# First attention of a float32 transformer: output projection in two parts, heads 0 to 5 and heads 6 to 7, with the attention's items in the order of the heads

## The chip, the cores and the metric

The kernel runs on one core of one Trainium2 chip, as one program. The metric is the time of an execution on the device, in microseconds (us); lower is better. The engines of the core are named as the profile names them: PE (TensorE, matrix products and transposes), DVE (VectorE), ACT (ScalarE), POOL (GpSimd), and SP, whose queue issues most of the transfers of weights.

## The reference, cut to what matters

A first block of two layers (a convolution layer, then an attention layer) is followed by a second block. All is float32, 512 positions of 1024 channels. The change lies in the attention layer of the first block: eight heads, each with two sets of scores whose softmaxes are subtracted; the 128 outputs of each head are normalised by their own root mean square; then comes the product with `w_o`, whose result is normalised again, scaled and added to x.

```python
    def one_block(args):                       # one of 4 blocks of 128 query positions
        ...
        s = jnp.einsum("bqhcd,bkhcd->bhcqk", q_blk, k).astype(jnp.float32) * scale + bias[None, :, None]
        s = jnp.where(rel >= 0, s, -jnp.inf)
        p = jax.nn.softmax(s, axis=-1)
        a = (p[:, :, 0] - lam * p[:, :, 1]).astype(v.dtype)
        return jnp.einsum("bhqk,bkhe->bqhe", a, v)
    o = lax.map(one_block, (q, starts))
    o = jnp.moveaxis(o, 0, 1).reshape(bsz, seq, N_HEADS, V_HEAD_DIM)
    o = rms_norm(o, subln_g) * (1.0 - lambda_init)
    return o.reshape(bsz, seq, N_HEADS * V_HEAD_DIM) @ w_o
...
        x = x + g_m * rms_norm(y, norm_g[l, 1])
        h = rms_norm(x, norm_g[l, 2]) * (1.0 + sc_f) + sh_f
        y = conv_ffn(h, ffn_w_in[l], ffn_dw[l], ffn_dwb[l], ffn_w_out[l])
```

## The kernel before, in words

Every large product is made of three: both factors are split into a high part and a low part, and `mm3` (L208) issues high by high, low by high and high by low, each 128x128 by 128x512. A weight comes in by a transfer on SP's queue (`wr`), ACT casts its high part (`wh`, L135), and DVE or, for every second piece here, POOL subtracts to get the low part (`wl`, L137).

The attention is a list of 32 items (`todo`), one for each head and query block (`qb`, also called a token block, 0 to 3). `pipeline` goes through it one item per iteration: it issues the scores of item i (`attn1_s`, PE `sc` L1160), then the first half of the filling work, the transposes of the probabilities of item i-2 (`attn1_t`, PE `aT` L1198, copied by ACT to `at`, L1200), the second half of the filling work, and the product with v of item i-4 (`attn1_v`, PE `pv` L1206, written to `o` by ACT L1208, its squares summed by L1209). The scores of item i+1 come next on PE. The statistics of an item are DVE's (maxima, L1170 to L1174), its exponentials are ACT's (L1177, L1179); the combination of the two softmaxes (DVE L1186 to L1190) is issued one iteration later. Query block 3 has four times the columns of query block 0.

The filling work is a list of generators, `fillers`; `fill` advances the first one so many steps per item, as `FILL1` sets it: 4.61, and 5 from item 26 on. A step is one `mm3`. The fillers are first the projections of heads 1 to 7 (`proj`: eight steps for k, whose sum DVE copies to `kq`, L1149, and eight for q, which ACT copies, L1151); then the output projection, `down8`. It takes token blocks 0 to 3 in turn, for each the two halves of the output columns (`acc`), eight steps each, one for each head's 128 channels of `o`.

For a token block whose last head is done, POOL computes the eight roots (`rstd_pool`, L202), and `advance` counts its steps (`age`): at `MULT` DVE multiplies `o` by them (L1259, 128x1024), at `AGE` PE transposes it (`T` in the words below, PE `ps` L351), ACT copies it with the gain (`hf`, L374), and DVE splits it into four pairs of high and low parts (`put`, L367 and L368). The items of heads 6 and 7 are interleaved so that head 7 begins early:

```python
    todo = [(hd, qb) for hd in range(6) for qb in range(4)]
    todo += [(6, 0), (6, 1), (7, 0), (6, 2), (7, 1), (6, 3), (7, 2), (7, 3)]
```

After the product a token block's rows are normalised and added to x (`norm_half` and `norm_end`, L386 to L400), give the new `xr` (L326), and are transposed and evacuated once more (`T` and `E`) as the input of the layer's feed-forward part. For that, x comes back from memory by four transfers of 512 KB (`reload`), issued when the first token block's heads are done.

Of the kernel before, what the change touches and what calls it, by code (L numbers as in the profile page):

```python
# [38 lines left out]
LALD2 = (7, 8)  # L39
LAG1 = (2, 4)  # L40
MID = 2
MULT = 4
FILL1 = (4.61, 5)
AGE = (9, 11, 6, 10, 14, 12, 21, 12)
SEL_RATE = (1.4, 1, 0.6, 0.4, 1.0, 1.3, 1.3, 1.0, 1.2)
SEL_TICK = 4
START_PAIRS = 3
# [644 lines left out]
def program(b, t, out, stop):  # L692
# [277 lines left out]
    def mk_chain(gb):  # L970

        def end(tok, ps):
            b.norm_end(tok, ps, gb())
            xr[tok] = b.xr_of(tok, ss=b.ssx[:, tok, :])
        return (lambda tok, ps: b.norm_half(tok, ps, gb())), end
# [61 lines left out]
    def run_ffn(l, E, h, bg, rate, chain, T2, E2):  # L1037

        units, inter = ffn(l, None)
        b.bg += bg  # L1040
        b.bgrate = rate
        b.start_units(units, h, T, E, first=3)
        b.bgrate *= 2
        b.down(inter, NF, ('fo', l), chain, T2, E2)
# [4 lines left out]
    def E_mod(h, l, ja, js):  # L1049
        def E(tok):  # L1050
            if tok == 0:
                b.finish(f'm{l}{ja}')
                b.finish(f'm{l}{js}')
            b.evac_mod(tp.pop(tok), tok, h, b.mod[l, ja], b.mod[l, js])
        return E
# [175 lines left out]
                    done(j)  # L1231
    for _ in proj(0):
        pass
    todo = [(hd, qb) for hd in range(6) for qb in range(4)]
    todo += [(6, 0), (6, 1), (7, 0), (6, 2), (7, 1), (6, 3), (7, 2), (7, 3)]
    sg = b.C([128, 1], n="sg")
    nc.vector.tensor_scalar(out=sg, in0=b.col('subln'), scalar1=1.0 - LINIT, scalar2=None, op0=ALU.mult)
    age, orr = {}, {}
    h = b.newpair(8)
    E = E_mod(h, 1, 4, 3)  # L1240

    def done(j):
        hd, tok = todo[j]
        if hd < 7:
            return
        if tok == 0:
            holder['oc'] = b.newpair(8)
            b.reload()
            fillers.append(b.down8(holder['oc'], 'wo', mk_chain(lambda: b.mod[1, 2]), T, E, pre=lambda tok: age.get(tok, 0) >= AGE[4 + tok]))
        orr[tok] = b.rstd_pool(oss[tok], 128, 8)  # L1250
        age[tok] = 0

    def advance():

        for tok in age:
            age[tok] += 1
            if age[tok] == MULT:
                oo = o[tok].rearrange("p (h e) -> p h e", e=128)
                nc.vector.tensor_tensor(out=oo, in0=oo, in1=orr[tok].unsqueeze(2).to_broadcast([128, 8, 128]), op=ALU.mult)  # L1259
            if age[tok] == AGE[tok]:  # L1260
                b.evac_gain(b.transp(o[tok]), tok, holder['oc'], sg)
        while fillers:
            try:
                next(fillers[0])
                return
            except StopIteration:
                fillers.pop(0)
# [2 lines left out]
    owed = [0.0]  # L1270

    def fill(i, part):
        owed[0] += FILL1[0] / 2 if i < 26 else FILL1[1] / 2
        while owed[0] >= 1:
            owed[0] -= 1
            advance()
# [12 lines left out]
        b.evac_gain(tp.pop(tok), tok, holder['h2'], ang2)  # L1289
    b.lo_pool = LO_POOL[1]  # L1290
    b.side = rel_bias2(b, t, tab)
    run_ffn(1, E, h, [('rope', rope_tables(b, t))], 1, mk_chain(lambda: b.mod[1, 5]), T, E_b2)
    assert next(b.side, 0) == 0
    b.side = None
    if stop == 'ffn1':
# [456 lines left out]
def rope_tables(b, t):  # L1752

    nc = b.nc
    posi = b.G([128, 512], I32, n="posi")
    nc.sync.dma_start(out=posi, in_=t['positions_2'][0].partition_broadcast(128))
    posf = b.G([128, 512], n="posf")
    nc.vector.tensor_copy(posf, posi)
    rc = b.C([128, 2], n="rc")
    nc.sync.dma_start(out=rc, in_=t['k_rope'])  # L1760
    yield

    ak_ = b.G([128, 2, 512], n="ang")
    ang, kk = ak_[:, 0, :], ak_[:, 1, :]
    nc.vector.tensor_scalar(out=ang, in0=posf, scalar1=rc[:, 0:1], scalar2=None, op0=ALU.mult)
    yield
    MAGIC = 12582912.0
    nc.vector.tensor_scalar(out=kk, in0=ang, scalar1=1.0 / (2 * math.pi), scalar2=MAGIC, op0=ALU.mult, op1=ALU.add)
    yield
    nc.vector.tensor_scalar(out=kk, in0=kk, scalar1=-MAGIC, scalar2=None, op0=ALU.add)  # L1770
    yield
    c1, c2 = 6.28125, 0.0019340515136718750
    c3 = 2 * math.pi - c1 - c2
    for cc in (c1, c2, c3):
        nc.vector.scalar_tensor_tensor(out=ang, in0=kk, scalar=-cc, in1=ang, op0=ALU.mult, op1=ALU.add)
    nc.vector.tensor_scalar(out=ang, in0=ang, scalar1=math.pi, scalar2=-math.pi, op0=ALU.min, op1=ALU.max)
    yield
    trig = b.G([128, 2, 512], n="trig")
    sin_t, cos_t = trig[:, 0, :], trig[:, 1, :]
    nc.scalar.activation(out=sin_t, in_=ang, func=AF.Sin)  # L1780
    yield
    nc.vector.tensor_scalar(out=sin_t, in0=sin_t, scalar1=rc[:, 1:2], scalar2=None, op0=ALU.mult)
    yield
    nc.vector.scalar_tensor_tensor(out=kk, in0=ang, scalar=-1.0, in1=ang, op0=ALU.mult, op1=ALU.max)
    nc.vector.tensor_scalar(out=kk, in0=kk, scalar1=-1.0, scalar2=math.pi / 2, op0=ALU.mult, op1=ALU.add)
    yield
    nc.scalar.activation(out=cos_t, in_=kk, func=AF.Sin)
    yield
    b.trig = sin_t, cos_t
    yield  # L1790
# [150 lines left out]
```

## Time and profile before

| | us |
|---|---|
| runs | 2046.29, 2044.12, 2044.9 |
| median | 2044.9 |
| profiled execution | 2047.63 |
| its span | 2045.9 |

The profile is of one execution, whose own time is the third row; the span is from its first to its last instruction. PE's busy time is 96% of the span, DVE's 62%, ACT's 41%, POOL's 8%, and the mean of the clock granted to PE is 0.984 of full speed. A timeline row gives the start, the duration, the engine, the line, the operation with what it writes and reads, and in square brackets the idle time of the engine ahead of it with what ended that. Where matmuls stand in a row, the duration of one reaches into the next: the starts say how fast they follow each other.

### The profile page before, as it was taken

Reading aid. Unit: us, or ns where it says so; the run is one execution under the profiler, and the core shown is the slowest. Engines: PE = TensorE matmul, PEld = TensorE weight load, DVE = VectorE, ACT = ScalarE, POOL = GpSimd, SP = SyncE. Lnnn points to the kernel's source line nnn. Section 1 sums busy time; section 2 is a strip of 40 time slices with the busy share of each in tenths; the row PEclk is TensorE's granted clock in tenths of the full one; section 3 lists DMA queues with packets and bytes.
Section 4 is the critical chain, followed back from the end, with each engine's and each line's share of the span. In section 5 each row is a group of like instructions: output and inputs, shape, how many; then the busy total and the mean of one; then the engine's idle time right before and its main releaser. Section 6 shows DMA issues by size and latency. Waiting matters only on the chain. (4 is left out here: it accounts for less than half of the span.)

```text
span 2045.9 us, 25689 instructions
## 1 busy us (share of the span) xinstructions
PE 1956.2 (96%) x9616; PEld 1612.2 (79%) x9618; DVE 1273.5 (62%) x2429; ACT 829.8 (41%) x1682; POOL 156.2 (8%) x99
## 2 busy tenths in 40 slices
PE   5999999999999999889999999989999999999998
PEld 3798788777887877678888888867777878888887
DVE  7788667777866665767766633668786646433432
ACT  3310454343424455745444422554445335322421
POOL 1201000000000111110000000022222100000000
PEclk9999899999999999999999999999999999999999
DMA  8375236443665311302932333321114433332221
GB/s 316 115 249 178 78 138 226 132 148 137 227 251 184 116 47 61 136 36 105 252 117 86 97 109 134 117 62 48 46 45 126 161 134 114 114 129 88 82 93 42
DMA packets 85418, 259.47 MB, mean 127 GB/s; under 512 B 9429, under 2 KB 21117, under 8 KB 85290
## 3 DMA queue, kind: packets, MB, share of 16 engines
q1 hardware_dynamic: 77802, 232.63, 34.4%
q10 hardware_dynamic: 7488, 25.17, 3.2%
q8 instruction: 76, 1.25, 0.2%
q14 instruction: 52, 0.43, 0.1%
HBM read 243.04 MB, written 23.64 MB: 130 GB/s over the span
## 5 line engine op out<-in xcount | busy, mean ns | idle before, releaser
L210 PE MATMUL up<-hh,wh 128*128 128x512 f32 (+1 forms) x1280 | 479.8, 375 | 5.2 <-ACT hh L769 2.1
L212 PE MATMUL up<-hh,wl 128*128 128x512 f32 (+1 forms) x1280 | 475.3, 371 | 4.0 <-DVE wl L137 3.8
L211 PE MATMUL up<-hl,wh 128*128 128x512 f32 (+1 forms) x1280 | 475.1, 371 | 1.2 <-DVE hl L771 1.0
L137 DVE TENSOR_TENSOR wl<-wr,wh 128x1024 fp32r<-128x1024 f32 x247 | 301.6, 1232 | 169.8 <-ACT wh L135 144.0
L135 ACT CAST wh<-wr 128x1024 fp32r<-128x1024 f32 (+2 forms) x308 | 307.9, 1020 | 181.9 <-DMA wr<-in_w_all_dram 97.4
L210 PEld LDWEIGHTS up<-hh,wh 128*128 128x128 f32 x1280 | 243.1, 190 | 50.7 <-issue 2.8
L212 PEld LDWEIGHTS up<-hh,wl 128*128 128x128 f32 x1280 | 243.1, 190 | 49.9 <-DVE wl L137 9.1
L211 PEld LDWEIGHTS up<-hl,wh 128*128 128x128 f32 x1280 | 243.1, 190 | 45.2 <-DVE hl L771 3.3
L210 PE MATMUL acc<-wh,ih 128*128 128x512 f32 x608 | 237.4, 390 | 0.0
L211 PE MATMUL acc<-wl,ih 128*128 128x512 f32 x608 | 236.8, 389 | 0.2 <-DVE wl L137 0.2
L212 PE MATMUL acc<-wh,il 128*128 128x512 f32 x608 | 236.6, 389 | 0.0
L137 POOL TENSOR_TENSOR wl<-wr,wh 128x1024 fp32r<-128x1024 f32 (+2 forms) x61 | 131.8, 2166 | 1002.0 <-ACT wh L135 845.7
L211 PEld LDWEIGHTS acc<-wl,ih 128*128 128x128 f32 x608 | 114.2, 188 | 24.3 <-DVE wl L137 0.9
L212 PEld LDWEIGHTS acc<-wh,il 128*128 128x128 f32 x608 | 114.1, 188 | 23.9
L210 PEld LDWEIGHTS acc<-wh,ih 128*128 128x128 f32 x608 | 114.1, 188 | 23.4
L263 DVE SCALAR_TENSOR_TENSOR macc<-mraw,cact,macc 128x1024 f32<-128x1024 f32 x74 | 95.2, 1287 | 8.5 <-DMA mraw<-in_mod_w_dram 7.8
L1028 ACT CAST ih<-fc 128x512 fp32r<-128x512 f32 x44 | 37.9, 861 | 142.7 <-DVE fc L1020 142.7
L996 ACT ACTIVATE fc<-up,cols 128x512 f32<-128x512 f32 x88 | 68.2, 775 | 37.3 <-PE up L212 37.3
L1001 DVE SCALAR_TENSOR_TENSOR fc<-up,cols,fc 128x384 f32<-128x384 f32 (+3 forms) x176 | 72.8, 479 | 4.7 <-ACT fc L996 4.7
L210 PE MATMUL unit<-hh,wh 128*128 128x512 f32 x152 | 72.3, 476 | 0.7 <-ACT kh L1405 0.5
L1012 ACT ACTIVATE fc<-fc 128x512 f32<-128x512 f32 x44 | 27.8, 632 | 102.3 <-DVE fc L1001 61.4
L1029 DVE TENSOR_TENSOR il<-fc,ih 128x512 fp32r<-128x512 f32 x44 | 39.8, 904 | 40.9 <-ACT ih L1028 40.9
(324 smaller groups left out, 3023.3 us busy)
## 6 DMA issues: line engine op xcount, KB each, us to landing
wr<-in_w_all_dram SPq DMA_DIRECT2D x282, 512.0 KB, 3.7
mraw<-in_mod_w_dram SPq DMA_DIRECT2D x80, 512.0 KB, 5.1
xd<-x ACTq DMA_DIRECT2D x20, 512.0 KB, 2.8
x<-xd ACTq DMA_DIRECT2D x20, 512.0 KB, 5.6
mraw<-in_w_all_dram SPq DMA_DIRECT2D x16, 512.0 KB, 9.6
wr<-in_w_all_dram SPq DMA_DIRECT2D x17, 256.0 KB, 2.7
wr<-in_w_all_dram SPq DMA_DIRECT2D x8, 384.0 KB, 9.5
sk<-fd SPq DMA_DIRECT2D x6, 512.0 KB, 15.8
```

The costliest lines, as they stand in the source:

```text
L135: self.nc.scalar.copy(hi, raw)
L137: (self.nc.gpsimd if pool else self.nc.vector).tensor_tensor(out=lo, in0=raw, in1=hi, op=ALU.subtract)
L210: mm(ps, lh, rh, start=start, stop=False)
L211: mm(ps, lh, rl, start=False, stop=False)
L212: mm(ps, ll, rh, start=False, stop=stop)
L263: nc.vector.scalar_tensor_tensor(out=acc, in0=raws[k], scalar=s, in1=acc, op0=ALU.mult, op1=ALU.add)
L996: nc.scalar.activation(out=o, in_=ps, func=AF.Identity, scale=dw[:, 88 + j:89 + j], bias=dwb[:, j:j + 1])
L1001: nc.vector.scalar_tensor_tensor(out=a, in0=e, scalar=dw[:, w + j:w + j + 1], in1=a, op0=ALU.mult, op1=ALU.add)
L1012: nc.scalar.activation(out=o, in_=o, func=AF.Silu)
L1028: nc.scalar.copy(hi, o)
L1029: nc.vector.tensor_sub(lo, o, hi)
```

## The change

The items go head by head. The filling work is 4.0 steps an item, and 3 from item 28 on. The output projection gets a generator of its own, `wo`, in place of `down8`. It is divided by heads: part 0 is heads 0 to 5, six of the eight steps of a sum, part 1 is heads 6 and 7. `WO_ORDER` lists token blocks 0 and 1 with part 0 (both halves of the columns, 24 steps), then their part 1, then token blocks 2 and 3 with all. The roots, the multiply (now at age 3), the transposes (at age 6), the copies and the pairs of a token block are made for each part by itself, for heads 0 to 5 as soon as head 5 is done for that token block. `WO_T` says before which of the parts the transposes of the new `xr` stand, and `h1`, the pair of tiles that they fill, is taken at the first of them. The reload of x is issued two iterations later.

```diff
@@ -39,9 +39,13 @@
 LALD2 = (7, 8)
 LAG1 = (2, 4)
 MID = 2
-MULT = 4
-FILL1 = (4.61, 5)
-AGE = (9, 11, 6, 10, 14, 12, 21, 12)
+MULT = 3
+FILL1 = (4.0, 3)
+HA = 6
+WO_ORDER = [(tok, half, part) for part in range(2) for tok in (0, 1) for half in range(2)]
+WO_T = {(2, 1, 0): 0, (2, 0, 1): 1, (3, 0, 1): 2}
+WO_ORDER += [(tok, half, part) for tok in (2, 3) for part in range(2) for half in range(2)]
+AGE = (6, 9)
 SEL_RATE = (1.4, 1, 0.6, 0.4, 1.0, 1.3, 1.3, 1.0, 1.2)
 SEL_TICK = 4
 START_PAIRS = 3
@@ -1231,34 +1235,86 @@
                     done(j)
     for _ in proj(0):
         pass
-    todo = [(hd, qb) for hd in range(6) for qb in range(4)]
-    todo += [(6, 0), (6, 1), (7, 0), (6, 2), (7, 1), (6, 3), (7, 2), (7, 3)]
+    todo = [(hd, qb) for hd in range(8) for qb in range(4)]
     sg = b.C([128, 1], n="sg")
     nc.vector.tensor_scalar(out=sg, in0=b.col('subln'), scalar1=1.0 - LINIT, scalar2=None, op0=ALU.mult)
     age, orr = {}, {}
-    h = b.newpair(8)
-    E = E_mod(h, 1, 4, 3)
+
+    def E(tok):
+        if tok == 0:
+            b.finish('m14')
+            b.finish('m13')
+            holder['h1'] = b.newpair(8)
+        b.evac_mod(tp.pop(tok), tok, holder['h1'], b.mod[1, 4], b.mod[1, 3])
+
+    def wo():
+
+        la, b.la = b.la, 0
+        ws = [b.get(('wo', 0, k0)) for k0 in range(0, 8, 2)]
+        oc, first, end = holder['oc'], *mk_chain(lambda: b.mod[1, 2])
+        ps = {}
+
+        def seg(tok, half, ks):
+            if ks[0] == 0:
+                ps[tok, half] = b.PS(n="acc")
+            for k in ks:
+                if len(ws) < 8 and k % 2:
+                    ws.append(b.get(('wo', 1, 2 * len(ws) - 8)))
+                w = ws[half * 4 + k // 2]
+                a, e = tok * 128, tok * 128 + 128
+                b.mm3(ps[tok, half], oc.hi(k, a, e), oc.lo(k, a, e), w[0][:, k % 2, :], w[1][:, k % 2, :], k == 0, k == 7)
+                yield
+        for tok, half, part in WO_ORDER:
+            while age.get((part, tok), 0) < AGE[1]:
+                yield
+            if tok == NT - 1 and half and part:
+                b.la = la
+            if tok >= 2 and not half and not part:
+                b.ahead(min(la, tok - 1))
+            if (tok, half, part) in WO_T:
+                T(WO_T[tok, half, part])
+                E(WO_T[tok, half, part])
+            yield from seg(tok, half, range(HA) if not part else range(HA, 8))
+            if part:
+                (end if half else first)(tok, ps.pop((tok, half)))
+        b.ahead()
 
     def done(j):
         hd, tok = todo[j]
-        if hd < 7:
-            return
-        if tok == 0:
-            holder['oc'] = b.newpair(8)
-            b.reload()
-            fillers.append(b.down8(holder['oc'], 'wo', mk_chain(lambda: b.mod[1, 2]), T, E, pre=lambda tok: age.get(tok, 0) >= AGE[4 + tok]))
-        orr[tok] = b.rstd_pool(oss[tok], 128, 8)
-        age[tok] = 0
+        if hd == HA - 1:
+            orr[0, tok] = b.rstd_pool(oss[tok][:, 0:HA], 128, HA)
+            age[0, tok] = 0
+        if hd == 7:
+            orr[1, tok] = b.rstd_pool(oss[tok][:, HA:], 128, 8 - HA)
+            age[1, tok] = 0
+            if tok == 0:
+                b.reload()
+
+    def heads(part, tok):
+        return (0, HA) if not part else (HA, 8)
 
     def advance():
 
-        for tok in age:
-            age[tok] += 1
-            if age[tok] == MULT:
-                oo = o[tok].rearrange("p (h e) -> p h e", e=128)
-                nc.vector.tensor_tensor(out=oo, in0=oo, in1=orr[tok].unsqueeze(2).to_broadcast([128, 8, 128]), op=ALU.mult)
-            if age[tok] == AGE[tok]:
-                b.evac_gain(b.transp(o[tok]), tok, holder['oc'], sg)
+        for part, tok in age:
+            age[part, tok] += 1
+            k0, k1 = heads(part, tok)
+            n = k1 - k0
+            if age[part, tok] == MULT:
+                oo = o[tok][:, k0 * 128:k1 * 128].rearrange("p (h e) -> p h e", e=128)
+                nc.vector.tensor_tensor(out=oo, in0=oo, in1=orr[part, tok].unsqueeze(2).to_broadcast([128, n, 128]), op=ALU.mult)
+            if age[part, tok] == AGE[0]:
+                if (part, tok) == (0, 0):
+                    holder['oc'] = b.newpair(8)
+                    fillers.append(wo())
+                a = slice(tok * 128, tok * 128 + 128)
+                hf = b.G([128, n, 128], n="hf")
+                for q, ps in enumerate(b.transp(o[tok][:, k0 * 128:k1 * 128], n)):
+                    m = min(4, n - 4 * q)
+                    nc.scalar.activation(out=hf[:, 4 * q:4 * q + m, :], in_=ps[:, :m, :], func=AF.Copy, scale=sg)
+                for q in range(n // 2):
+                    hi, lo = holder['oc'].his[k0 // 2 + q][:, :, a], holder['oc'].los[k0 // 2 + q][:, :, a]
+                    nc.vector.tensor_copy(hi, hf[:, 2 * q:2 * q + 2, :])
+                    nc.vector.tensor_sub(lo, hf[:, 2 * q:2 * q + 2, :], hi)
         while fillers:
             try:
                 next(fillers[0])
@@ -1270,7 +1326,7 @@
     owed = [0.0]
 
     def fill(i, part):
-        owed[0] += FILL1[0] / 2 if i < 26 else FILL1[1] / 2
+        owed[0] += FILL1[0] / 2 if i < 28 else FILL1[1] / 2
         while owed[0] >= 1:
             owed[0] -= 1
             advance()
@@ -1289,7 +1345,7 @@
         b.evac_gain(tp.pop(tok), tok, holder['h2'], ang2)
     b.lo_pool = LO_POOL[1]
     b.side = rel_bias2(b, t, tab)
-    run_ffn(1, E, h, [('rope', rope_tables(b, t))], 1, mk_chain(lambda: b.mod[1, 5]), T, E_b2)
+    run_ffn(1, E, holder['h1'], [('rope', rope_tables(b, t))], 1, mk_chain(lambda: b.mod[1, 5]), T, E_b2)
     assert next(b.side, 0) == 0
     b.side = None
     if stop == 'ffn1':
```

The first place is ACT at the end of a head's items. Before, these are the rows around the copy of q of head 4 (`kq_6084`); `p` with 128x256 x2 are the exponentials of query block 1, the rows with 128x128 and 128x256 those of query block 2, `wh` is a weight's cast.

```order
L1179 ACTIVATE p_6210,sm_6209<-p_6210,sm_6208 128x256 x2
L1200 COPY at_6235<-aT_6230 128x512
L1151 ACTIVATE kq_6084<-kp_6183 128x512
L1208 ACTIVATE o_5506<-pv_6244,sm_6019 128x128
L1209 ACTIVATE junk_83,oss_5510<-pv_6244,sm_6019 128x128
L1177 ACTIVATE p_6256,sm_6255<-sc_6249,sm_6254 128x128
L1179 ACTIVATE p_6256,sm_6255<-p_6256,sm_6254 128x256
L1177 ACTIVATE p_6256,sm_6255<-sc_6251,sm_6254 128x128
L1179 ACTIVATE p_6256,sm_6255<-p_6256,sm_6254 128x256
L135 CAST wh_6272<-wr_6089 128x1024
```

After, the rows that end with the copy of q of head 6 (`kq_6518`) begin with the exponentials of query block 2, and those with 128x256 from `sc_6642` and `sc_6644` are of query block 3.

```order
L1181 ACTIVATE p_6598,sm_6597<-sc_6593,sm_6596 128x128
L1183 ACTIVATE p_6598,sm_6597<-p_6598,sm_6596 128x256
L139 CAST wh_6613<-wr_6426 128x1024
L1204 COPY at_6628<-aT_6626 128x128
L1212 ACTIVATE o_5507<-pv_6636,sm_6417 128x128
L1213 ACTIVATE junk_83,oss_5511<-pv_6636,sm_6417 128x128
L1181 ACTIVATE p_6649,sm_6648<-sc_6642,sm_6647 128x256
L1183 ACTIVATE p_6649,sm_6648<-p_6649,sm_6647 128x256
L1181 ACTIVATE p_6649,sm_6648<-sc_6644,sm_6647 128x256
L1183 ACTIVATE p_6649,sm_6648<-p_6649,sm_6647 128x256
L1204 COPY at_6674<-aT_6671 128x256
L1155 ACTIVATE kq_6518<-kp_6619 128x512
```

The copy of q has moved from behind the exponentials of query block 1 to behind those of query block 3, the last item of the head before; the cast stands behind those of query block 2 in both.

The second place is DVE between query blocks 2 and 3 of a head's items. Before (head 4's; `p_6410` is the combination of query block 1):

```order
L1174 TENSOR_SCALAR sm_6459<-sm_6458 128x2
L1187 RECIPROCAL sm_6416<-sm_6409 128x2
L1189 SCALAR_TENSOR_TENSOR sm_6473<-sm_6409,sm_6416,nlam_2173 128x1
L1190 SCALAR_TENSOR_TENSOR p_6410<-p_6410,sm_6473 128x256
L1170 TENSOR_REDUCE sm_6505<-sc_6501 128x1
L1171 ISA p_6508,sm_6505<-sc_6501,bt_5515,sm_6505 128x256
```

After (the items of head 5, with `wl_6614` the low part of a weight):

```order
L1178 TENSOR_SCALAR sm_6596<-sm_6595 128x2
L1191 RECIPROCAL sm_6561<-sm_6554 128x2
L1193 SCALAR_TENSOR_TENSOR sm_6610<-sm_6554,sm_6561,nlam_2173 128x1
L1194 SCALAR_TENSOR_TENSOR p_6555<-p_6555,sm_6610 128x256
L141 TENSOR_TENSOR wl_6614<-wr_6426,wh_6613 128x1024
L1174 TENSOR_REDUCE sm_6646<-sc_6642 128x1
L1175 ISA p_6649,sm_6646<-sc_6642,bt_5515,sm_6646 128x256
```

The low part of a weight now stands between the combination and the maxima of query block 3.

The third place is PE from the first transposes of `o` on. Before, `ps_7055` and `ps_7060` are those of token block 0; the last scores are `sc_6995` and `sc_6997`, and the first product of the output projection is `acc_7092`.

```order
L1160 MATMUL sc_6995<-kq_6619 128x512
L1160 MATMUL sc_6997<-kq_6619 128x512
L1198 MATMUL aT_7030<-ident_71,p_6918 128x128 x4
L1206 MATMUL pv_7038<-v_5087,at_6937 128x128
L1206 MATMUL pv_7038<-v_5088,at_6937 128x128
L1206 MATMUL pv_7038<-v_5089,at_6937 128x128
L1198 MATMUL aT_7049<-ident_71,p_6951 128x128 x3
L351 MATMUL ps_7055<-ident_71,o_5505 128x128 x4
L351 MATMUL ps_7060<-ident_71,o_5505 128x128 x4
L1206 MATMUL pv_7076<-v_5087,at_6970 128x128
L1206 MATMUL pv_7076<-v_5088,at_6970 128x128
L1198 MATMUL aT_7084<-ident_71,p_7002 128x128 x4
L210 MATMUL acc_7092<-wh_6528,hh_6976 128x512
```

After, the transposes of token block 0 (six, for heads 0 to 5) stand in the third item of head 6 (`sc_6789`), and `kp_6817` is head 7's projection:

```order
L1164 MATMUL sc_6789<-kq_6518 128x384
L1164 MATMUL sc_6791<-kq_6518 128x384
L214 MATMUL kp_6817<-hh_5079,wh_6519 128x512
L215 MATMUL kp_6817<-hl_5083,wh_6519 128x512
L216 MATMUL kp_6817<-hh_5079,wl_6520 128x512
L355 MATMUL ps_6830<-ident_71,o_5505 128x128 x4
L355 MATMUL ps_6835<-ident_71,o_5505 128x128 x2
L214 MATMUL kp_6817<-hh_5079,wh_6519 128x512
```

The first products of the output projection stand after the first scores of head 7 (`sc_6938`), with the transposes of token block 2 among them:

```order
L1210 MATMUL pv_6928<-v_5090,at_6771 128x128
L1164 MATMUL sc_6938<-kq_6709 128x128
L1164 MATMUL sc_6940<-kq_6709 128x128
L214 MATMUL acc_6969<-wh_6613,hh_6821 128x512
L215 MATMUL acc_6969<-wl_6614,hh_6821 128x512
L216 MATMUL acc_6969<-wh_6613,hl_6825 128x512
L1202 MATMUL aT_6973<-ident_71,p_6796 128x128 x3
L355 MATMUL ps_6980<-ident_71,o_5507 128x128 x4
L355 MATMUL ps_6985<-ident_71,o_5507 128x128 x2
L214 MATMUL acc_6969<-wh_6613,hh_6821 128x512
L215 MATMUL acc_6969<-wl_6614,hh_6821 128x512
```

The transposes of `o` for six heads and the first products now stand among the scores of heads 6 and 7; before, all of them stood behind the last scores.

## Rows read from the trace of the kernel before

**Rows 1.** The page, part 1: busy time, share of the span, instructions.
```profile
PE 1956.2 (96%) x9616; PEld 1612.2 (79%) x9618; DVE 1273.5 (62%) x2429; ACT 829.8 (41%) x1682; POOL 156.2 (8%) x99
```

**Rows 2.** Windows: busy PE, PEld, DVE, ACT, POOL; PEclk; DMA share; GB/s.
```profile
724.70:801.70 77.00, 76.07 (x378) 56.21 (x378) 48.72 (x157) 46.41 (x156) 12.00 (x5) 1.00 0.16 52
...
841.60:860.00 18.40, 14.35 (x89) 9.48 (x89) 15.24 (x69) 16.33 (x72) 0.00 (x0) 1.00 0.33 117
860.00:870.00 10.00, 6.44 (x29) 5.49 (x28) 8.80 (x23) 8.76 (x27) 6.11 (x5) 0.68 0.94 359
...
890.00:900.00 10.00, 5.60 (x19) 4.52 (x18) 6.29 (x15) 3.55 (x8) 0.00 (x0) 0.71 0.13 52
...
sum 205.40, PE 190.81 PEld 146.53 DVE 132.11 ACT 126.28 POOL 35.16; mean PE 21.20 PEld 16.28 DVE 14.68 ACT 14.03 POOL 3.91
```

**Rows 3.** Timeline of PE: waits, and products behind the transposes of o.
```profile
742.21 0.49 PE L1160 MATMUL sc<-kq 64*128 64x128 f32 x4 [0.91 <-ACT kq L1151]
...
864.35 1.97 PE L351 MATMUL ps<-ident,o 128*128 128x128 f32 x8 [1.39 <-DVE o L1259]
...
883.41 1.06 PE L351 MATMUL ps<-ident,o 128*128 128x128 f32 x8 [1.66 <-DVE o L1259]
...
889.57 0.39 PE L212 MATMUL acc<-wh,hl 128*128 128x512 f32 x1
...
890.25 0.39 PE L212 MATMUL acc<-wh,hl 128*128 128x512 f32 x1
...
895.03 1.94 PE L351 MATMUL ps<-ident,o 128*128 128x128 f32 x8 [4.40 <-DVE o L1259]
...
904.04 0.39 PE L212 MATMUL acc<-wh,hl 128*128 128x512 f32 x1
...
937.09 1.09 PE L351 MATMUL ps<-ident,xr 128*128 128x128 f32 x8 [1.06 <-DVE xr L326]
```

**Rows 4.** Timeline of PE: scores of heads 5 and 6.
```profile
821.97 0.49 PE L1160 MATMUL sc<-kq 64*128 64x128 f32 x4
...
825.92 0.70 PE L1160 MATMUL sc<-kq 64*128 64x256 f32 x4
...
831.11 0.92 PE L1160 MATMUL sc<-kq 64*128 64x384 f32 x4
...
836.38 1.13 PE L1160 MATMUL sc<-kq 64*128 64x512 f32 x4
...
841.55 0.49 PE L1160 MATMUL sc<-kq 64*128 64x128 f32 x4
```

**Rows 5.** Timeline of ACT: last exponentials of a head, and the copies.
```profile
741.48 0.20 ACT L1179 ACTIVATION_READ_ACCUMULATOR p<-p,sm 128x1 f32 x1
...
741.58 0.59 ACT L1151 ACTIVATE kq<-kp 128x512 f32<-128x512 f32 x1
...
742.05 0.37 ACT L1200 COPY at<-aT 128x256 f32<-128x256 f32 x1
...
841.98 0.19 ACT L1179 ACTIVATION_READ_ACCUMULATOR p<-p,sm 128x1 f32 x1
```

**Rows 6.** Timeline of DVE: low part, maxima, multiply, first and last of put.
```profile
836.93 1.23 DVE L137 TENSOR_TENSOR wl<-wr,wh 128x1024 fp32r<-128x1024 f32 x1 [1.57 <-ACT wh L135]
...
838.07 0.42 DVE L1170 TENSOR_REDUCE sm<-sc 128x1 f32<-128x256 f32 x1
...
864.60 2.00 DVE L1189 SCALAR_TENSOR_TENSOR sm<-sm,sm,nlam 128x1 f32<-128x1 f32 x1
...
882.05 1.22 DVE L1259 TENSOR_TENSOR o<-o,sm 128x1024 f32<-128x1024 f32 x1
...
884.80 0.29 DVE L367 CAST hh<-hf 128x256 fp32r<-128x256 f32 x1 [0.93 <-ACT hf L374]
...
887.12 0.42 DVE L368 TENSOR_TENSOR hl<-hf,hh 128x256 fp32r<-128x256 f32 x1
```

**Rows 7.** Timeline of POOL: a low part beside the DVE row at 864.60.
```profile
864.22 2.36 POOL L137 TENSOR_TENSOR wl<-wr,wh 128x1024 fp32r<-128x1024 f32 x1 [1.19 <-ACT wh L135]
```

## The prediction

> **What bounds the kernel now.** I read the page first: TensorE (PE) is busy for 1956.2 us of the span, 96% [rows 1]. PE work is the same before and after (the same 192 output-projection products and 32 transposes), so the time can only move by what PE waits for and by the clock that it is granted. The windows over the attention come next: from the first scores at 724.7 to the last product of the output projection at 930.1 there are 205.4 us with 190.81 of PE busy, so 14.6 us of waiting; the heads up to 801.7 run at clock 1.00, while 860 to 870 has 0.68 and 890 to 900 has 0.71 [rows 2]. The PE timeline then shows where. One wait of 0.91 us lies at the boundary between heads 0 and 1, where the scores wait for ACT's copy of q; the others, 14.6 - 0.91 = 13.7 us, all lie between 846 and 895, the largest at the transposes of o (1.39, 1.66, 4.40 us), each behind DVE's normalising multiply L1259 [rows 3].
>
> The clock costs something besides. After the wait of 1.66 us the eight transposes and 23 further products take 889.57 - 883.41 = 6.16 us; after the wait of 4.40 the same work takes 904.04 - 895.03 = 9.01 [rows 3]. That is 2.85 us per fall, and there are two falls (the transposes at 864.35 take 1.97, not 1.06). So the tail loses 13.7 + 5.7 = 19.4 us now, and that is all the change can win there.
>
> **The change, part by part.** *Head by head, four steps an item.* One step is three matmuls, 890.25 - 889.57 = 0.68 us [rows 3]. A head's q and k need 16 steps, an item now gets exactly 4, a head has 4 items: each head's last step falls at the very end of the item ahead of its first scores. Before, at 4.61 steps, the projections ran further and further ahead of the first scores that need them (at 841.55, those of head 6, nothing waits [rows 4]). So from now on every one of the boundaries of heads 1 to 7 has the pattern that stood only at 742.21 before: the scores wait for ACT's copy of q, and ACT has that copy behind the exponentials of the last item of the old head. I price it from the item that has the new order of DVE and ACT already, the one starting at 836.38. DVE has the low part of a weight split (L137) there, starting at 836.93 and giving way at 838.07, ahead of the item's maxima [rows 6]; the last exponential's read starts at 841.98 [rows 5]. At 742 the read began at 741.48, the copy at 741.58, the scores at 742.21: 0.73 us from read to scores, and the copy of a^T, which after stands between them, takes about 0.3 (0.37 in its row, 0.25 to the next start) [rows 5]. Scores would then start at 841.98 + 0.73 + 0.3 = 843.0, where PE was free at 841.55: 1.45 us. The item before it had 5 steps, now it has 4, so PE comes 0.68 earlier, while the chain of exponential, cast, low part and maxima hangs on the scores of 831.11 and does not move: **2.1 us** per boundary, for heads 2 to 6 10.5 us. The new order puts that low part in front of the last item's maxima in every head. Head 1 has no pv products as cover and two steps fewer (18 of 4.61 became 16): PE is free at 742.21 - 0.91 - 1.36 = 739.94, the scores at 742.58 (with the a^T copy) or 743.7 (with the low part's 1.14 in the path too): 2.6 to 3.8, I take 3.2. Sum 13.7 us, where before had 0.91. Lower bound: without the low part in the way (its 1.14 us), 0.95 each and 2.6, together 7.4; the row of 0.91 is near that, but it had no low part in its last item.
>
> *Norms and projection in two parts.* Multiplies shrink from eight blocks (1.22 us, row at 882.05) to six (about 0.9) and two (0.3); three of four put pairs come with the first part, where four take 887.12 + 0.42 - 884.80 = 2.74, so 0.68 a pair [rows 6]. They now stand among the statistics of items 26 to 29, on DVE, which each item waits for. I walk it from the first scores of head 6 (time 0). Items without waits take 3.95, 5.19 - 0.68, 5.27 - 0.68 and 5.17 us [rows 4], plus 0.6 for six transposes (an estimate: eight take 1.06 [rows 3], and the next product starts ahead of their end). Item 26 starts at 8.5, 27 at 13.7, and PE comes to the transposes of token 1 at 15.4. On DVE the low part waits for the cast behind the exponentials of item 26 (from the scores at 831.11 to the low part at 836.93 is 5.8 [rows 4, 6], so it starts at 14.3), and gives way at 15.4; three pairs of token 0 go until 17.4, the multiply of token 1 until 18.2: PE waits **2.8**. Only then come the maxima and exponentials of item 27 (838.07 to some 842.0 in the old rows, 4.0: until 22.2), the evacuation of token 1 (estimated 0.9, six blocks), a^T and q (0.25 + 0.6: until 23.95), where PE is free at 13.7 + 5.17 + 0.6 + 2.8 = 22.25: **1.7** at the boundary of head 7. Token 2's transposes wait 0.35. The pairs of token 2 meet POOL's low part (2.36 us, [rows 7]) and a low part of DVE's own follows, so token 3's multiply ends some 4.0 after PE comes to its transposes: **4.0**. The first product with the weight that POOL splits there waits 1.2, and a^T of item 29, whose maxima were pushed back by the same queue, 2.5 (both from the same walk). Items 32 to 35 then fit: the 24 steps of tokens 0 and 1 on heads 0 to 5 cover the exponentials that left PE waiting from 846 to 863. The three transposes of the new x wait 0.2, 1.3 and 0.4 (near the 1.06 at 937.09, [rows 3]); the last, of token 3, is as before. Sum 2.8 + 1.7 + 0.35 + 4.0 + 1.2 + 2.5 + 1.9 = **14.5 us** (14.45).
>
> That a POOL subtract holds DVE up is in the rows: a DVE operation on one column takes 2.00 us at 864.60 beside POOL's subtract from 864.22 [rows 6, 7]. If DVE were free there, token 3 would wait 1.9 less and my sum with it. The Trainium skill, page "SBUF — State Buffer", section "Who interferes with whom", says that a VectorE instruction with two SBUF inputs and a GpSimd one that reads SBUF shut each other out for the whole instruction; by that rule the 4.0 stands, and the trace agrees.
>
> *Clock.* Before, falls followed 4.40 and the close group of waits that ends at 864.35; the single 1.66 at 883.41 and 0.91 at 742.21 were followed by full level (the transposes took 1.06). Token 3's 4.0 is the nearest to the 4.40, and a fall after it costs 2.85 at most; I take 2 us, between 0 and 5.7.
>
> *Moved at no price.* Four POOL roots and four multiplies more are on engines that wait anyway once items 32 to 35 are reached. The four 512 KB reloads of x move from iteration 30 to 32 of the item loop; before, they and the output weights filled the DMA from 860 to 870 (share 0.94, [rows 2]). What hides them is the four iterations and the remaining steps ahead of the first norm end, 20 steps or 14 us at least; if that cover went, token 0's transposes would be late by at most those 10 us.
>
> **Sum.** Waits 13.7 + 14.5 = 28.2 against 14.6: +13.6; clock 2.0 against 5.7: -3.7. Change +9.9 us against the profiled execution's 2047.63 us, so 2057.5 in its own terms; the median of the runs is 2044.9, 2.7 lower, and the same step gives **2054.8**.
>
> **Rivals.** *Faster: the early products cover the tail.* If DVE keeps up (multiply and pairs in the holes of 26 to 29, no fall of the clock), all 19.4 are won and only the boundaries stay: 13.7 - 0.91 - 19.4 = -6.6, so 2038.3. For it: 24 steps are 16 us of PE work where 13.7 us of waiting were. Against it: the waits shown hang on DVE, and the change puts more on DVE in just the items that have the longest maxima. It decides once tail waits and clock together stay under 2.5 us (20.3 in all now, less 13.7, less the 4.1 that can be told).
> *Same: short boundaries.* If the cast comes early enough for the low part to pass before the maxima, boundaries are 7.4, the rest as walked: +3.6, so 2048.5. Against it: the row at 836.93, where DVE waited 1.57 us for the cast in just this place.
> *Slower still: the clock falls at every boundary.* Seven falls of 2.85 are 20 us on top of +9.9: 2074.8. Against it: 0.91 and 1.66 brought no fall; for it: boundaries of 2 to 3 us lie between these and 4.40. The Trainium skill, page "TensorE: Matmul & The Clock Gate", section "A second HAM failure mode: psum-queue depth-cycling", says that frequent short idling between groups of matmuls makes the clock swing between its levels; that would be this rival, and the clock of 1.00 from 724.7 to 801.7 with its wait of 0.91 doesn't show it.
> That the change fails to do what it says is not a case: the new order of PE has the first products of six heads in item 28.
>
> **How the numbers follow.** Chances: my forecast 0.57, the covered tail 0.17, short boundaries 0.18, the falling clock 0.08. A difference of about 0.2% (4.1 us) is what a measurement of this kernel can tell. Faster by more: the covered tail, 0.17. Within: short boundaries, and 0.04 from the forecast's low end, 0.22. Slower: 0.61. The forecast's own range takes head 1 (0.6 either way), the clock (-2, +3.7) and some 3 us either way for the tail's walk: 2050 to 2061. The range with the cases takes in all but the lower half of the covered tail, about 0.09, and the falling clock: 2040 to 2064.
>
> **What would show it.** The first scores of heads 1 to 7 each with a wait of 1.5 to 3.8 us behind ACT's copy of q (under 1 us: the short boundaries are right). In the item of those waits DVE's low part directly before the maxima. Transposes of tokens 1 and 3 with waits of 2 to 4 us behind the multiply. Nearly no PE wait from item 32 until the transposes of the new x. Clock 1.00 up to head 6, one fall at most behind it. The prediction is wrong if items 26 to 31 show less than 3 us of waiting, or if the clock is under 0.95 in the heads.

## The result, and the profile after

| | median us | runs | lowest to highest |
|---|---|---|---|
| before | 2044.9 | 5 | 2044.12 to 2046.29 |
| after | 2055.43 | 5 | 2052.2 to 2058.6 |

The ratio is 1.0056, with a 95% interval of 1.0044 to 1.0068: the change makes the kernel slower by 10.5 us. The prediction was 2054.8 us, with a range from 2040 to 2064.

The profiled execution after the change is the slowest of the five, 2058.6 us (span 2056.8), so its own difference to the one of before is 10.9 us of span. PE's work is the same, as the page says (it answers to [rows 1]):

```profile
PE 1957.4 (95%) x9618; PEld 1611.4 (78%) x9618; DVE 1269.0 (62%) x2433; ACT 830.8 (40%) x1686; POOL 157.8 (8%) x107
```

The timeline of PE, with every row from the first scores of head 0 to the transposes of the new x that has a wait in front of it (it answers to [rows 3]):

```profile
720.61 0.49 PE L1164 MATMUL sc<-kq 64*128 64x128 f32 x4 [0.69 <-ACT kq L1155]
...
739.53 0.49 PE L1164 MATMUL sc<-kq 64*128 64x128 f32 x4 [3.71 <-ACT kq L1155]
...
761.14 0.49 PE L1164 MATMUL sc<-kq 64*128 64x128 f32 x4 [1.78 <-ACT kq L1155]
...
781.24 0.49 PE L1164 MATMUL sc<-kq 64*128 64x128 f32 x4 [1.83 <-ACT kq L1155]
...
801.28 0.49 PE L1164 MATMUL sc<-kq 64*128 64x128 f32 x4 [1.75 <-ACT kq L1155]
...
821.36 0.49 PE L1164 MATMUL sc<-kq 64*128 64x128 f32 x4 [1.86 <-ACT kq L1155]
...
843.06 0.49 PE L1164 MATMUL sc<-kq 64*128 64x128 f32 x4 [1.83 <-ACT kq L1155]
...
861.31 0.85 PE L355 MATMUL ps<-ident,o 128*128 128x128 f32 x6 [2.52 <-DVE o L1304]
...
866.94 0.56 PE L1164 MATMUL sc<-kq 64*128 64x128 f32 x4 [1.60 <-ACT kq L1155]
...
868.89 0.84 PE L355 MATMUL ps<-ident,o 128*128 128x128 f32 x6 [0.17 <-DVE o L1304]
...
877.77 1.51 PE L355 MATMUL ps<-ident,o 128*128 128x128 f32 x6 [3.77 <-DVE o L1304]
...
888.88 0.41 PE L1202 MATMUL aT<-ident,p 128*128 128x128 f32 x2 [0.58 <-DVE p L1194]
...
894.15 0.52 PE L1202 MATMUL aT<-ident,p 128*128 128x128 f32 x3 [1.89 <-DVE sm L1190]
...
921.70 1.09 PE L355 MATMUL ps<-ident,xr 128*128 128x128 f32 x8 [0.93 <-DVE xr L330]
...
934.10 1.06 PE L355 MATMUL ps<-ident,xr 128*128 128x128 f32 x8 [0.38 <-DVE xr L330]
...
937.52 0.39 PE L216 MATMUL acc<-wh,hl 128*128 128x512 f32 x1
```

The reader is to see two families. Six waits at the first scores of heads 1 to 6 sum to 12.76 us; there was 0.91 before. The waits from 861 on sum to 11.84, where before had 13.7. So the stretch has 24.6 us of waits instead of 14.6; the wait at 866.94, of the second family by its place, is at the first scores of head 7. From 720.61 to the end of the last product (the next instruction starts 0.23 us behind 937.52) the stretch lasts 217.1 us, against 205.4 [rows 2].

Without its waits and the two falls of the clock the stretch took 205.4 - 14.6 - 5.7 = 185.1 us before; the same work leaves 217.1 - 185.1 - 24.6 = 7.4 us after. The three falls of the clock that the windows show take 6.2 of them: 1.7 each behind the first scores of heads 1 and 5 (rows in the last section), and 12 times 0.23, or 2.8, from 878 to 890. So the 11.7 us are 10.0 of waits, about 0.5 of clock, and 1.2 that are in neither. PE's busy time in the stretch has grown by about as much as the last two together (192.4 us, from 190.81). One reason may be that a product in front of a wait counts with its whole 0.39 or 0.40 us, where otherwise the next one starts after 0.23, and that more waits stand behind a product now; that this is all of the 1.2 is not shown.

The windows show where the clock was lost (columns as in [rows 2]):

```profile
200.00:300.00 100.00, 93.04 (x522) 77.98 (x521) 67.56 (x160) 50.75 (x116) 6.27 (x10) 0.97 0.34 123
...
720.60:801.20 80.60, 71.60 (x349) 52.24 (x349) 43.12 (x156) 45.57 (x157) 9.54 (x4) 0.98 0.15 46
801.20:843.00 41.80, 38.09 (x188) 28.52 (x188) 21.37 (x80) 24.27 (x88) 4.75 (x2) 0.96 0.16 51
...
878.00:890.00 12.00, 11.42 (x46) 7.88 (x46) 8.93 (x28) 7.00 (x22) 2.35 (x1) 0.77 0.14 44
...
1400.00:1600.00 200.00, 188.75 (x1001) 153.68 (x1001) 148.82 (x513) 91.96 (x278) 47.96 (x27) 0.95 0.23 67
```

Of the kernel before, three rows to hold beside them:

```profile
200.00:300.00 100.00, 93.03 (x487) 77.64 (x486) 65.03 (x155) 49.00 (x114) 6.29 (x10) 0.90 0.34 123
...
801.70:841.60 39.90, 39.90 (x206) 30.15 (x205) 22.34 (x81) 24.59 (x88) 4.76 (x2) 1.00 0.19 60
...
1400.00:1600.00 200.00, 188.54 (x1063) 153.81 (x1064) 150.95 (x523) 96.82 (x294) 49.33 (x28) 0.99 0.26 73
```

The heads, which ran at 1.00 before, are at 0.98 and 0.96 now. The stretches from 200 and from 1400 are of work that the change doesn't touch; their clock differs between the two executions all the same. With that goes that the attention starts 4.1 us earlier in this execution than in the profiled one of before, and that what follows its last product is 3.3 us longer (1119.1 against 1115.8 us); -4.1 + 11.7 + 3.3 makes the 10.9.

The mechanism at a boundary reads off ACT and DVE ahead of the scores at 821.36. The item of query block 2 starts its scores at 809.71, that of query block 3 at 814.31. ACT, from the cast on (it answers to [rows 5]):

```profile
814.19 1.03 ACT L139 CAST wh<-wr 128x1024 fp32r<-128x1024 f32 x1
...
818.56 0.47 ACT L1181 ACTIVATE p<-sc,sm 128x256 f32<-128x256 f32 x1 [2.55 <-DVE sm L1190]
...
820.36 0.19 ACT L1183 ACTIVATION_READ_ACCUMULATOR p<-p,sm 128x1 f32 x1
820.45 0.36 ACT L1204 COPY at<-aT 128x256 f32<-128x256 f32 x1
820.71 0.60 ACT L1155 ACTIVATE kq<-kp 128x512 f32<-128x512 f32 x1
```

And DVE (it answers to the first two of [rows 6]):

```profile
815.31 1.23 DVE L141 TENSOR_TENSOR wl<-wr,wh 128x1024 fp32r<-128x1024 f32 x1 [2.06 <-ACT wh L139]
816.45 0.42 DVE L1174 TENSOR_REDUCE sm<-sc 128x1 f32<-128x256 f32 x1
```

DVE stands idle for 2.06 us, waiting for the cast; then the low part keeps the maxima until 816.45; ACT then waits 2.55 us for the maxima, and the copy of q is the last thing in the line. No engine is busy for long here; a chain of five steps has no lead.

### The profile page after: what moved, and what is told of

It is laid out like the page before. It is cut to its first block, busy times and chain, and to the rows that moved or that the text cites. A ratio compares the mean times of both kernels' runs of the same rounds, so it can differ in the third digit from the quotient of the medians.

```text
span 2056.8 us, 25709 instructions
## 1 busy us (share of the span) xinstructions
PE 1957.4 (95%) x9618; PEld 1611.4 (78%) x9618; DVE 1269.0 (62%) x2433; ACT 830.8 (40%) x1686; POOL 157.8 (8%) x107
## 3 DMA queue, kind: packets, MB, share of 16 engines
q8 instruction: 76, 1.25, 0.2%
```

## The experiments

Two theories stand against each other. **A**: the waits at the heads come from a copy without lead (ACT's order, and DVE's low part in front of it), and the waits from 861 on from DVE's queue. **B**: the engines need that time anyway, or the loss lies in the divided projection. The kernel before ran again beside the experiments, and the ratios are to those runs: its median was 2043.69 us beside the first three below and the one with later transposes, 2043.62 beside the last two, and 2043.57 beside the others.

**Lead of one item.** Each head's projection no longer ends with the step ahead of its first scores, but four steps earlier. The first product of the output projection moves ahead with it, from item 28 to item 27.

```diff
-    owed = [0.0]
+    owed = [4.0]
```

> The changed kernel with the projections one item (four steps) ahead: the counter of owed steps starts at 4, nothing else differs. Theory A (the scores of each new head wait because ACT's copy of q stands behind the last exponentials of the old head, with no lead): the waits of 1.75 to 3.71 us at the first scores of heads 1 to 7 fall under 0.3 us each, 14.4 us in all, and little comes back, so about 2043 us (2040 to 2046). Rival B (DVE and ACT need that time anyway, the boundary only shows where PE stands still): the waits turn up at the transposes of the probabilities instead, and the time stays at 2053 to 2056.

Measured: 2044.27 us, ratio to before 1.0004 (0.9994 to 1.0013). The waits of its PE timeline behind the first scores of head 0, up to the last of o:

```profile
721.49 0.49 PE L1164 MATMUL sc<-kq 64*128 64x128 f32 x4 [0.69 <-ACT kq L1155]
...
847.61 0.85 PE L355 MATMUL ps<-ident,o 128*128 128x128 f32 x6 [1.42 <-DVE o L1304]
...
861.04 1.51 PE L355 MATMUL ps<-ident,o 128*128 128x128 f32 x6 [7.75 <-DVE o L1304]
...
877.17 2.07 PE L1164 MATMUL sc<-kq 64*128 64x512 f32 x2 [1.65 <-ACT p L1181]
...
893.82 0.41 PE L355 MATMUL ps<-ident,o 128*128 128x128 f32 x2 [1.18 <-DVE o L1304]
```

All seven boundary waits are gone, none has come back within the heads, and the time is that of before. So A holds for the heads. What remains up to the last transposes of o is 12.0 us in four waits. The longest, 7.75 us, stands behind the multiply, at the transposes of token block 2; the experiments on the tail below take it up.

**The rate alone, on the kernel before.** Nothing of the division, of the order of items or of the norms.

```diff
-        owed[0] += FILL1[0] / 2 if i < 26 else FILL1[1] / 2
+        owed[0] += (2.0 if i < 20 else 2.67) if i < 26 else FILL1[1] / 2
```

> The kernel before with one part of the change alone: 4.0 steps an item for the first 20 items, so that heads 1 to 5 get their last step just ahead of their first scores, then 5.34 an item up to item 26; order of items, output projection and norms as before. Theory A: waits of about 3.7 us at head 1 and 1.8 at heads 2 to 5 where there was 0.91 in all, so +10 us, 2055 (2052 to 2058). Rival B' (the loss comes from the divided projection and its norms, not from the rate): 2044 to 2047.

Measured: 2055.76 us, ratio 1.0063 (1.0046 to 1.0081); the waits at heads 1 to 5 are 3.71, 1.80, 1.85, 1.76 and 1.85. The rate by itself costs what the whole change costs, and rival B' is out.

**The copy of q on DVE.**

```diff
-                nc.scalar.activation(out=qt[hd], in_=p, func=AF.Copy, scale=0.125)
+                nc.vector.tensor_scalar(out=qt[hd], in0=p, scalar1=0.125, scalar2=None, op0=ALU.mult)
```

> The changed kernel with the copy of q on DVE instead of ACT (one tensor_scalar of 128x512). Theory A: the copy no longer stands behind the exponentials but behind the combination of query block 2, which ends about 5.5 us after the last scores of the old head, where PE is free after 5.1; with 0.7 us for the copy the waits of 1.8 become about 1.1, that of 3.7 about 2.5, and the time 2049 to 2051. If the low part on DVE, and not the exponentials, sets the copy, the waits stay within 0.3 us of what they are, and the time at 2054 to 2056.

Measured: 2052.25 us, ratio 1.0046 (1.003 to 1.0063). The waits at heads 2 to 6 are 0.77 to 0.88, at head 1 2.61; but at head 7, where DVE has multiplies and pairs, the copy now waits in DVE's queue:

```profile
860.85 0.49 PE L1164 MATMUL sc<-kq 64*128 64x128 f32 x4 [4.16 <-DVE kq L1155]
```

It was 1.60. Of some 6 us won at heads 1 to 6, 2.6 go back there; ACT's order is half of the boundary wait. The time came out above the 2049 to 2051 that were expected; the 2.6 us at head 7 are as much as is missing.

**The low part one item later.** ACT's order stays, and the subtraction is issued behind the maxima.

```diff
+        def low():
+            (self.nc.gpsimd if pool else self.nc.vector).tensor_tensor(out=lo, in0=raw, in1=hi, op=ALU.subtract)
...
+            self.defer.append(low)
...
     def fill(i, part):
+        if not part:
+            for low in b.defer or ():
+                low()
+            b.defer = [] if i < 24 else None
```

> The changed kernel with the low part of each weight's split issued one item later in the heads up to item 23, so that it stands behind the maxima and the combination instead of in front of the maxima of query block 3. Theory A (the low part's 1.14 us on DVE is the second part of the wait, the order of ACT the first): the waits of 1.75 to 1.86 us fall to 0.6 to 0.9, that of 3.71 to about 2.6, the time to 2048 to 2051. Rival (the exponentials alone set it, DVE has room): waits and time as they are, 2053 to 2057.

Measured: 2048.58 us, ratio 1.0025 (1.0016 to 1.0035). Its PE timeline at heads 1, 2 and 6:

```profile
739.57 0.49 PE L1170 MATMUL sc<-kq 64*128 64x128 f32 x4 [1.77 <-ACT kq L1161]
...
758.71 0.49 PE L1170 MATMUL sc<-kq 64*128 64x128 f32 x4 [0.88 <-ACT kq L1161]
...
835.25 0.49 PE L1170 MATMUL sc<-kq 64*128 64x128 f32 x4 [0.89 <-ACT kq L1161]
```

The low part is worth 0.9 to 1.0 us at the boundaries of heads 2 to 6 (its place on DVE is 816.45 - 815.31 = 1.14) and 1.94 at head 1, where DVE's wait for the cast counts too. What is left at heads 2 to 6, 0.84 to 0.89, is about the wait of 0.91 that stood at 742.21 before [rows 3]. This was the lower bound of the prediction, and the rival of the short boundaries.

**The early products held back.** The first products of heads 0 to 5 then stand behind the last scores.

```diff
-AGE = (6, 9)
+AGE = (6, 26)
```

> The changed kernel with the early products held back: they wait for age 26 instead of 9, so that items 28 to 31 have no steps of the output projection and the first of its products stands behind the last scores, as before the change. Theory A (the early products fill time in which PE waits for DVE and ACT anyway): the waits from item 28 to the end of the items grow by 3 to 8 us, and the time to 2058 to 2063. Rival (the products only push the waits on and win nothing): 2053 to 2057.

Measured: 2063.63 us, ratio 1.0102 (1.0084 to 1.0121), 8.2 us above the changed kernel and just above the range expected. Its waits from the transposes of token block 1 to the last transposes of o are 2.54, 1.59, 0.91, 4.15, 2.05, 1.80 and 3.16, together 16.2, against 10.5 with the products. So the early products do cover 5.7 us of waits. That is not all of the 8.2: PE has five falls of the clock in this stretch, where the changed kernel has three. The division's idea works; it isn't what makes the kernel slower.

**Transposes of o two steps later.**

```diff
-AGE = (6, 9)
+AGE = (8, 11)
```

> The changed kernel with the transposes of o two steps later (age 8 instead of 6, products from age 11 instead of 9). Theory A (PE comes to the transposes of token blocks 1 and 3 ahead of DVE's multiply): their waits of 2.52 and 3.77 us shrink by about 1.4 us each, since DVE's multiply stays where it is, and the time is 2051 to 2054. Rival (DVE as a whole is behind in items 26 to 30, so the wait moves to the next item's maxima and transposes): the sum of the waits from item 26 to 31, 10.5 us, stays within 1 us, and the time too.

Measured: 2057.25 us, ratio 1.0067 (1.0051 to 1.0084). The wait at token block 1's transposes is gone, and the PE timeline has it elsewhere:

```profile
867.25 0.87 PE L1164 MATMUL sc<-kq 64*128 64x128 f32 x4 [4.25 <-ACT kq L1155]
...
885.52 1.96 PE L1164 MATMUL sc<-kq 64*128 64x512 f32 x4 [2.26 <-ACT p L1181]
```

The sum from item 26 to 31 is 4.25 + 0.77 + 0.74 + 2.26 + 1.90 = 9.9, against 10.5. Here my reading failed and the rival held for the waits: the transposes were not too early; DVE and ACT as a whole are behind in these items, and where PE waits for them is a matter of order. The time is not within 1 us of the changed kernel's, as the rival said, but 1.8 above it; the intervals of the two ratios overlap.

**Less for DVE in the tail.** On the kernel with the lead, first the low parts of the output weights on DVE instead of every second on POOL, then the high parts of the pairs of o on ACT instead of DVE.

```diff
         la, b.la = b.la, 0
+        b.lo_pool = 0
```

```diff
-                    nc.vector.tensor_copy(hi, hf[:, 2 * q:2 * q + 2, :])
+                    nc.scalar.copy(hi, hf[:, 2 * q:2 * q + 2, :])
```

> The projections one item ahead, as in the first of these runs (2044.3 us), and in addition the low parts of the output projection's weights on DVE, none on POOL. Theory A (POOL's subtract holds DVE's pairs up, 1.96 and 2.52 us for operations of 0.29 and 0.42): the wait of 7.75 us at the third transposes falls by about 1.5 us (3.8 of holding up go, two low parts of 1.14 come), and the time is 2041 to 2044. Rival (DVE's own load in those items is all that counts): the wait grows by 2.3 us and the time to 2045 to 2048.

> The projections one item ahead (2044.3 us), and in addition the high parts of the pairs of o copied by ACT, not DVE: about 1.0 us less for DVE and 1.1 more for ACT per token block and part. Theory A (DVE's queue in items 26 to 29 is what PE waits for): the waits at the transposes of o, 1.42, 7.75, 1.18 and at the scores 1.65, together 12.0 us, fall by 2 to 4 us and the time to 2040 to 2043. Rival (ACT's queue is as full): they stay, 2043 to 2046.

Why the first should matter shows in the DVE timeline of the kernel with the lead, ahead of its wait of 7.75 us:

```profile
853.04 1.96 DVE L1316 CAST hh<-hf 128x256 fp32r<-128x256 f32 x1 [2.48 <-ACT hf L1313]
...
855.70 2.52 DVE L1317 TENSOR_TENSOR hl<-hf,hh 128x256 fp32r<-128x256 f32 x1
...
858.46 0.42 DVE L1317 TENSOR_TENSOR hl<-hf,hh 128x256 fp32r<-128x256 f32 x1
858.81 1.22 DVE L141 TENSOR_TENSOR wl<-wr,wh 128x1024 fp32r<-128x1024 f32 x1
859.94 0.95 DVE L1304 TENSOR_TENSOR o<-o,sm 128x768 f32<-128x768 f32 x1
```

and in its POOL timeline:

```profile
852.50 2.35 POOL L141 TENSOR_TENSOR wl<-wr,wh 128x1024 fp32r<-128x1024 f32 x1 [3.86 <-ACT wh L139]
855.60 2.34 POOL L141 TENSOR_TENSOR wl<-wr,wh 128x1024 fp32r<-128x1024 f32 x1 [0.75 <-ACT wh L139]
```

The two long DVE rows lie beside the two POOL rows and end at 855.00 and 858.22, just behind the ends of those (854.85 and 857.94); the same operations take 0.29 and 0.42 us otherwise. Measured: with the low parts on DVE 2040.18 us, ratio 0.9985 (0.9975 to 0.9994), and the wait is 4.55 instead of 7.75, though DVE has two more subtractions, and the casts and subtractions ahead of it take 0.29 and 0.42 us again. The waits of PE up to the last transposes of o sum to 9.8 us instead of 12.0. So Theory A held here, with a larger gain than expected.

With the high parts on ACT the time is 2039.98 us, ratio 0.9985 (0.9975 to 0.9994). That is as fast as Theory A said, but not by its mechanism: the four waits fall by 1.25 us only, to 10.75, not by 2 to 4, and the longest is still 6.82. POOL's second subtract now lies beside DVE's multiply, which takes 3.09 us instead of 0.95. Most of the 4.8 us that this execution wins between the first scores and the last product is clock. The lead alone has

```profile
870.00:880.00 10.00, 8.35 (x31) 4.69 (x30) 7.03 (x21) 5.10 (x19) 2.38 (x1) 0.85 0.00 0
880.00:890.00 10.00, 10.00 (x48) 8.23 (x48) 3.18 (x12) 4.76 (x17) 0.89 (x2) 0.81 0.17 54
```

a fall of 10 times (0.15 + 0.19), or 3.4 us, behind the wait of 1.65, and with the high parts on ACT there is none behind the wait of 1.58:

```profile
870.00:890.00 20.00, 17.21 (x89) 13.19 (x89) 9.46 (x31) 12.57 (x47) 4.93 (x7) 1.00 0.30 101
```

Whether the other nine executions won their time in the same way is not shown.

**All three, and all three with later transposes.**

> The three edits that helped, together: projections one item ahead, the low parts of the output projection's weights on DVE, the high parts of the pairs of o on ACT. If they take away separate parts of DVE's queue (Theory A), their gains of 4.1 and 4.3 us against 2044.3 add up to a good part: 2036 to 2039, some 5 to 7 us under the kernel before. If both only shorten the one wait at the third transposes and the next wait takes its place: 2039 to 2041.

> The same three edits with the transposes of o two steps later (age 8, products from age 10). Theory A (with DVE relieved, the transposes come too early for the multiply, and the steps ahead of them have room): 1 to 3 us less than the three edits alone. Rival (as in the run with age 8 on the changed kernel, DVE's queue is the bound and the wait only moves): within 1 us of it or slower.

Measured: 2039.86 us, ratio 0.998 (0.997 to 0.9989), and 2040.91 us, ratio 0.9983 (0.9974 to 0.9992). The gains don't add; the rival held both times. The wait at token block 2's transposes is down to 4.21 in the first, but one of 1.43 has come up at token block 3's. In the second, seven waits of 0.5 to 1.9 stand among scores, transposes and products, six of them behind ACT and one behind DVE. With the lead of one item and either edit on the tail, the change beats the kernel before by some 3 to 4 us, 0.2%; more was not found.

## Why the prediction was right

- **Boundaries of heads 2 to 6**: 2.1 us each was expected, 1.75 to 1.86 measured. From the last read of the exponentials to the scores it is 821.36 - 820.36 = 1.00 us, as worked out (1.03). The rest is the low part, which started 815.31 - 809.71 = 5.60 us after the scores of query block 2, not 5.82: in the row that I used, ACT had a copy of a^T ahead of the cast.
- **Head 1**: 3.2 expected between 2.6 and 3.8; 3.71. With the low part issued later it is 1.77, so the low part, with DVE's wait for its cast, was fully on the path.
- **The tail**: walked at 14.5 us, measured 11.84. The four at the transposes of o and at head 7 were right in place and size: 2.8, 1.7, 0.35 and 4.0 against 2.52, 1.60, 0.17 and 3.77. The 1.2 us for POOL's low part didn't come; the 2.5 us at the transposes of item 29's probabilities came as 0.58 there and 1.89 one item on; of the new x's 1.9 us, 1.31 came.
- **That POOL holds DVE up**: seen again in the run with the lead, 1.96 and 2.52 us for operations of 0.29 and 0.42, and removed by taking the subtractions from POOL.
- **The clock** is the term that was mis-sized: 2.0 us expected, with an upper bound of 5.7; 6.2 us in the profiled execution, and 1.2 more that are neither wait nor clock, for which the prediction had no term. I priced a fall behind token block 3's transposes only. It came (the six transposes at 877.77 take 1.51 us, those at 868.89 0.84), but two more came at the boundaries of heads 1 and 5, where the prediction had said a clock of 1.00. The rival "the clock falls at every boundary" was right in kind and wrong in number.
- **How much of it is luck**: the sign, the place of the waits and their sum of 24.6 against 28.2 us are not. That the median came out within 0.7 us of the forecast is: waits 3.6 us too high and clock and rest 5.4 too low nearly cancelled. The profiled execution is also the slowest of the five, and in the others, at clocks of 0.984 to 0.989 over the span, the clock's share differs.
- **The faster rival** failed at its condition: tail waits and clock together had to stay under 2.5 us, and the waits alone were 11.84. The run with the products held back shows that the products do cover 5.7 us of waits, as that rival says; against it stands, as the prediction had it, that the norms, pairs and multiplies for them came into the same items on DVE.

## What to carry to other kernels

When filling work has a product that the main work waits for, count the lead in steps, and then look at which instructions its last copy is queued behind on its engine: a rate that comes out exactly has no lead, and an offset of a few steps gives one without a higher rate. Work that is moved forward to cover waits brings its preparation with it; if the engine of the preparation is the one that PE already waits for, the wait changes its place and not its sum. Where only the order within a full queue is changed, as with the later transposes here, expect nothing; where the queue has holes, as at the heads, the order was worth 0.9 us and more at each boundary.

## What the runs showed of the hardware

Waits of the same length were followed by a fall of the granted clock in some places and not in others. The windows of 8 us behind the first scores of heads 1 to 6 in the changed kernel show it:

```profile
739.53:747.53 8.00, 8.00 (x35) 6.11 (x36) 3.47 (x17) 3.73 (x12) 2.38 (x1) 0.79 0.16 44
761.14:769.14 8.00, 8.00 (x42) 6.28 (x43) 3.46 (x17) 5.03 (x17) 2.37 (x1) 1.00 0.00 0
781.24:789.24 8.00, 8.00 (x42) 6.28 (x43) 3.46 (x17) 5.02 (x17) 2.39 (x1) 1.00 0.01 2
801.28:809.28 8.00, 8.00 (x42) 6.29 (x43) 3.46 (x17) 5.03 (x17) 2.38 (x1) 1.00 0.04 7
821.36:829.36 8.00, 8.00 (x34) 6.16 (x35) 3.46 (x17) 4.29 (x15) 2.37 (x1) 0.79 0.00 0
843.06:851.06 8.00, 8.00 (x42) 6.27 (x43) 4.19 (x18) 5.01 (x17) 3.91 (x3) 1.00 0.23 66
```

The waits are 3.71, 1.78, 1.83, 1.75, 1.86 and 1.83; PE was at its full level before each of them; behind the first and the fifth a part of the 8 us was at the lower one (2.4 and 1.2 GHz are the two), which costs 8 times 0.21, or 1.7 us. The same windows were read in five other profiles, those of the rate alone, the copy on DVE, the later transposes, the held products and the later low part. Of all boundaries with waits of 3.70 to 3.72 us 4 in 4 were followed by a fall, of those with 1.75 to 1.87 4 in 20, the one with 2.61 too, and of those with 0.77 to 0.89 none in 10. Which of the middle ones falls differs between executions (head 5 in three, head 3 in one); what decides it stays open. The Trainium skill, page "TensorE: Matmul & The Clock Gate", section "A second HAM failure mode: psum-queue depth-cycling", tells of a clock that swings between its levels when PE idles briefly and often; the trace agrees in part: of these boundaries, a fall followed all five waits of 2.61 us and more, four of the twenty of about 1.8, and none of the ten below 0.9.
